# Attention outputs with queries as rows: P blocks stationary, V with a ones column moving, division per row, PE turns into the mix

## The chip, the cores and the metric

The kernel runs one decoder layer on one Trainium2 chip, on 8 cores; each core computes one of the eight sequences and the cores do not talk to each other. The metric is the device time of the slowest core, in microseconds (us). Some executions in this case were in a second, slower state: the cores of one die (cores 0 to 3 or 4 to 7) showed a lower granted clock and the time grew (one run of the kernel before took 3652.38 us with a clock of 0.81 on cores 4 to 7, beside 3125.60 us in the same job). Such runs are told as slow here and compared with nothing.

Names used below: PE is TensorE (matmuls), PEld its weight loads, DVE VectorE, ACT ScalarE, POOL GpSimd. "N" is the number of columns that a matmul streams. "FoX" is the forgetting attention, "SWA" the sliding-window attention. The "granted clock" is the share of its full speed at which PE was allowed to run, as the trace records it. A "bank" is a piece of PSUM, the memory that PE writes its sums to.

## The reference, cut to what matters

```python
D_MODEL = 2048; BATCH = 8; SEQ = 2048; HEAD_DIM = 128      # per core: one sequence of 2048
# 8 FoX heads (causal, all earlier keys), 8 SWA heads (window 128, 2 kv heads, a sink logit)

def forgetting_attention(q, k, v, log_f):
    cum = cumsum(log_f)
    for i in range(S // 128):                               # blocks of 128 queries
        s = q_i @ k[:end].T * d**-0.5 + cum_q - cum_k       # causal mask
        out_i = softmax(s) @ v[:end]

def sliding_window_sink_attention(q, k, v, sinks):
    # each 128-query block reads its own and the previous key block
    p = softmax(concat([s, sink]))[..., :-1]
    out = p @ v

def reference(x, c, ...):
    h = rmsnorm(x) * (1 + sc) + sh;  proj = h @ w_in         # q, k, v of both groups, forget gates
    mix = concat([fox, swa]) @ w_out
    x = x + gt_a * rmsnorm(mix)
    y = square(relu((rmsnorm(x) * ...) @ w_up)) @ w_down     # the MLP, d_ff = 8192
    return x + gt_m * rmsnorm(y)
```

## The kernel before: the parts that the change touches

Every operation is recorded by small helpers (`pe`, `act`, `tt`, `cp`), which put semaphores where one engine's operation depends on another's. Each engine gets its operations in the order in which they were recorded. `F.fill(n)` records about n matmuls of other work (the projections of later heads) in between, so that PE has something to do while DVE and ACT make probabilities.

Scores are made with keys as rows: `P[k, q]`. In the kernel before, V is stationary and P moves, so an output tile has the head dimension as rows, which is the form that `mix` and the output projection want. The denominators come from a second matmul, with a matrix of ones as the stationary operand.

```python
    def pv(st):                                      # FoX, one step: 128 keys x up to 512 queries
        ...
        pe([mm(ob(c0, TS), v, pp, kb == 0, kb == nkb - 1), mm(db(c0, TS), ones(), pp, kb == 0, kb == nkb - 1)],
           [v, pp, ones()], [ob(), db()])
        if kb == nkb - 1:                            # the tile is done: divide
            os = accs[1]
            act(rr(), db(), AF.Ln)
            cp(os(), ob())
            act(rr(), rr(), AF.Exp, scale=-1.0)
            tt(mix(h, slice(j * TS, j * TS + TS)), os(), rr(), ALU.mult)

        for kb in range(16):                         # SWA, one pass of 4 heads, 16 blocks of queries
            sexp(kb, 0)                              # ACT: P from the scores of two heads
            sexp(kb, 1)
            if late:
                late()                               # normalise the block before: ACT Ln, Exp; DVE product
            F.fill(tot / 32)
            if kb + 1 < 16:
                sqk(kb + 1, 0)                       # PE: the next block's scores
                sqk(kb + 1, 1)
            F.fill(tot / 32)
            late = spv(kb)                           # PE: P.V and denominators; DVE: + sink
        late()
```

The scores of FoX use three PSUM banks in rotation (`SF`) and run three steps ahead of P.V; the scores of SWA use two (`SB`).

The softmax here doesn't subtract the row's maximum and nothing guards it: scores larger than these inputs give would overflow.

## Time and profile before

| | before |
|---|---|
| median of the first 3 runs | 3128.81 us (3125.04 to 3580.78; the highest is a slow run) |
| profiled run | 3126.5 us; spans of the cores 3109.0 to 3124.7 us |
| PE busy | 93% of the span |
| MLP from its first matmul (mean of the cores) | 1822.7 us |

The first lines are from the page of the kernel before: the span, the busy time of the engines, and the chain of work that ended last (the operations that each had to wait for the one before, followed back from the end).

```profile
span 3124.7 us, 38905 instructions; the slowest of 8 cores (3109.0 to 3124.7 us)
PE 2913.8 (93%) x15016; PEld 1375.2 (44%) x15016; DVE 928.1 (30%) x1489; ACT 748.4 (24%) x1224; POOL 469.1 (15%) x614
PE 82%; DVE 5%; DMA 4%; ACT 4%; issue 3%; POOL 1%; SPq 0%; DVEq 0%; ACTq 0%; POOLq 0%
```

So PE bounds this kernel. The next lines are a table of stretches of the kernel before: each row is a stretch of time, its length, the busy time of each engine with the number of instructions, and then the granted clock of PE as a share of full speed, the share of DMA time, and GB/s. The rows are FoX heads 0 and 1, the two SWA passes, FoX heads 2 to 7, and the MLP.

```profile
core 3: us, PE busy (x) PEld busy (x) DVE busy (x) ACT busy (x) POOL busy (x), PEclk, DMA share, GB/s
269.90:596.10 326.20, 290.20 (x1656) 138.85 (x1653) 147.97 (x244) 112.07 (x200) 25.36 (x48) 0.91 0.49 86
596.10:715.60 119.50, 116.72 (x849) 76.39 (x848) 50.01 (x78) 72.61 (x131) 8.12 (x16) 0.99 0.39 66
715.60:1081.60 366.00, 334.68 (x2009) 168.31 (x2007) 196.15 (x343) 184.47 (x309) 29.37 (x49) 0.96 0.46 84
1301.60:3124.70 1823.10, 1774.81 (x8205) 803.76 (x8203) 323.41 (x476) 219.32 (x365) 255.78 (x350) 0.99 0.53 104
```

The SWA passes are the densest stretch of the attention: PE is busy for 116.7 of 119.5 us. The timeline of the kernel before shows why (start, duration, engine, operation with output and input tiles and shapes; a number in brackets is idle time before it, and what ended it). One block of SWA:

```profile
start us, us, engine line op out<-in xcount [idle before <-releaser]
605.93 1.03 PE L387 MATMUL bank<-hT,ring_70 128*128 128x512 bf16 x4
606.71 0.69 DVE L407 TENSOR_TENSOR mix<-bank,qrot 128x512 bf16<-128x512 f32 x1 [1.54 <-ACT qrot L404]
607.22 0.28 PE L387 MATMUL bank<-Pb_102,vts 128*128 128x256 bf16 x1
...
608.00 0.27 PE L387 MATMUL bank<-Pb_99,ones 128*128 128x256 bf16 x1
608.11 1.03 PE L387 MATMUL bank<-hT,ring_70 128*128 128x512 bf16 x4
608.38 0.69 DVE L407 TENSOR_TENSOR rr<-bank,esink 128x512 f32<-128x512 f32 x1 [0.97 <-PE bank L387]
```

P·V begins at 607.22, the last denominator matmul at 608.00, and at 608.11 PE is already on a projection (`hT`, `ring`). The division happens on DVE and ACT beside it, and nothing on PE waits for it. Matmuls overlap, so their durations do not add up; read their starts: N=256 matmuls start every 0.11 us, each shown as 0.27 us long.

### The profile page before, as it was taken

How to read it: one execution, taken by the hardware profiler on the slowest of the kernel's cores; microseconds unless marked ns; L12 is line 12 of the kernel's file. 1: busy time of each engine (PE TensorE's matmuls, PEld its weight loads, DVE VectorE, ACT ScalarE, POOL GpSimd, SP SyncE). 2: the span in 40 equal slices, each digit the busy share in tenths (PEclk: the TensorE clock that was granted, in tenths of full speed). 3: DMA queues.
4: the chain of work that ended last, by engine and by line, in shares of the span. 5: the costliest groups of instructions: out<-in, count | busy, mean ns of one | idle time of the engine just before them, and what ended most of it. 6: DMA issues, size and time to landing. Idle time of an engine off the chain costs nothing.

```text
span 3124.7 us, 38905 instructions; the slowest of 8 cores (3109.0 to 3124.7 us)
## 1 busy us (share of the span) xinstructions
PE 2913.8 (93%) x15016; PEld 1375.2 (44%) x15016; DVE 928.1 (30%) x1489; ACT 748.4 (24%) x1224; POOL 469.1 (15%) x614
## 2 busy tenths in 40 slices
PE   2799989999999899999999999999999999999993
PEld 1336533466444344444444444444444444444441
DVE  1323445345555456642111000000233211000005
ACT  1312333454555435532111000000111111000000
POOL 1010000000001155520000011111100000111114
PEclk9899989999999899999999999999999999999996
DMA  9855545433646324354444455555788544444455
GB/s 185 215 90 104 101 75 88 78 61 59 112 85 102 77 95 157 127 130 74 78 78 74 82 100 95 96 92 96 162 189 191 92 75 78 77 75 77 78 99 197
DMA packets 99782, 327.92 MB, mean 105 GB/s; under 512 B 12144, under 2 KB 12272, under 8 KB 93200
## 3 DMA queue, kind: packets, MB, share of 16 engines
q0 software_dynamic: 58896, 213.97, 41.6%
q1 hardware_dynamic: 40704, 111.46, 10.2%
q8 instruction: 122, 2.00, 0.3%
q14 instruction: 60, 0.49, 0.1%
HBM read 497.32 MB, written 42.01 MB: 173 GB/s over the span
## 4 chain that ended last, share of the span: by engine, by line
PE 82%; DVE 5%; DMA 4%; ACT 4%; issue 3%; POOL 1%; SPq 0%; DVEq 0%; ACTq 0%; POOLq 0%
PE bank L387 82%; DVE bank L407 1%; POOL acc_209 L407 1%; DMA xstA<-xP 1%; DMA xstB<-xP 1%; DMA rmod_87<-wMA 1%; ACT acc_208 L404 1%; DVE mixF L412 1%; ACT rr L404 1%; DMA cfb_82<-crow 1%; ACT qrot L404 1%; DMA rsh_90<-wMB 0%; DVE bank L412 0%; DVE sq_207 L412 0%; DVE acc_208 L412 0%
## 5 line engine op out<-in xcount | busy, mean ns | idle before, releaser
L418 DVE TENSOR_SCALAR bank<-bank 128x512 f32<-128x512 f32 x256 | 166.1, 695 | 638.4 <-PE bank L387 638.4
L421 DVE COPY mixF<-bank 128x512 f32<-128x512 f32 x64 | 41.3, 686 | 842.8 <-PE bank L387 842.8
L387 PE MATMUL bank<-mix,rung_130 128*128 128x512 bf16 x1024 | 226.2, 379 | 0.0
L387 PE MATMUL bank<-mix,rung_127 128*128 128x512 bf16 x1024 | 226.2, 379 | 0.0
L387 PE MATMUL bank<-mix,rung_128 128*128 128x512 bf16 x1024 | 226.2, 379 | 0.0
L387 PE MATMUL bank<-mix,rung_129 128*128 128x512 bf16 x1024 | 226.2, 379 | 0.0
L404 ACT ACTIVATE sq_206<-bank 128x512 f32<-128x512 f32 x30 | 17.9, 598 | 792.9 <-DVE mixF L421 792.9
L387 PEld LDWEIGHTS bank<-mix,rung_129 128*128 128x128 bf16 x1024 | 100.2, 98 | 121.5 <-issue 1.1
L387 PEld LDWEIGHTS bank<-mix,rung_127 128*128 128x128 bf16 x1024 | 100.3, 98 | 120.7
L387 PEld LDWEIGHTS bank<-mix,rung_128 128*128 128x128 bf16 x1024 | 100.4, 98 | 120.7
L387 PEld LDWEIGHTS bank<-mix,rung_130 128*128 128x128 bf16 x1024 | 99.9, 98 | 121.5 <-issue 0.6
L407 DVE TENSOR_TENSOR bank<-bank,cfb_82 128x512 f32<-128x512 f32 x192 | 117.3, 629 | 85.2 <-PE bank L387 80.6
L387 PE MATMUL bank<-hT,ring_69 128*128 128x512 bf16 x512 | 139.6, 404 | 3.2 <-DVE sq_207 L412 3.2
L387 PE MATMUL bank<-hT,ring_71 128*128 128x512 bf16 x384 | 101.7, 394 | 0.4 <-DVE kT_73 L421 0.4
L407 POOL TENSOR_TENSOR acc_208<-acc_208,sq_206 128x512 f32<-128x512 f32 x62 | 78.6, 1267 | 113.1 <-ACT sq_206 L404 113.0
L407 DVE TENSOR_TENSOR bank<-bank,cfb_80 128x512 f32<-128x512 f32 (+3 forms) x128 | 73.5, 594 | 39.2 <-PE bank L387 39.2
L407 POOL TENSOR_TENSOR acc_209<-acc_209,sq_207 128x512 f32<-128x512 f32 x62 | 78.3, 1262 | 45.0 <-ACT sq_207 L404 43.1
L387 PE MATMUL bank<-qT_93,kT_94 128*128 128x512 bf16 (+3 forms) x160 | 57.4, 359 | 24.3 <-DVE bs L421 14.2
L387 PEld LDWEIGHTS bank<-hT,ring_69 128*128 128x128 bf16 x512 | 51.0, 103 | 61.3 <-issue 16.9
L387 PE MATMUL bank<-qT_72,kT_73 128*128 128x512 bf16 (+3 forms) x160 | 57.1, 359 | 18.9 <-DVE bs L421 8.8
L387 PE MATMUL bank<-hT,ring_68 128*128 128x512 bf16 x256 | 67.1, 394 | 1.1 <-DVE kT_73 L421 1.1
L387 PE MATMUL bank<-hT,ring_67 128*128 128x512 bf16 x192 | 58.9, 393 | 0.0
(759 smaller groups left out, 4803.5 us busy)
## 6 DMA issues: line engine op xcount, KB each, us to landing
rung_127<-wU POOLq DMA_DIRECT2D x32, 512.0 KB, 5.3
rung_128<-wU POOLq DMA_DIRECT2D x32, 512.0 KB, 5.3
rung_129<-wU POOLq DMA_DIRECT2D x32, 512.0 KB, 5.2
rung_130<-wU POOLq DMA_DIRECT2D x32, 512.0 KB, 5.4
rung_127<-wD POOLq DMA_DIRECT2D x32, 512.0 KB, 5.2
rung_128<-wD POOLq DMA_DIRECT2D x32, 512.0 KB, 5.3
rung_129<-wD POOLq DMA_DIRECT2D x32, 512.0 KB, 5.3
rung_130<-wD POOLq DMA_DIRECT2D x32, 512.0 KB, 5.7
```

What stands on the lines that cost most here:

```text
L387: ins = e.matmul(o, lhsT=l, rhs=rh, start=st, stop=sp)
L404: return P.op("act", lambda e: e.activation(out=out.ap, in_=in_.ap, func=func, **kw), r, [out])
L407: return P.op(eng, lambda e: e.tensor_tensor(out=out.ap, in0=a.ap, in1=b.ap, op=op), [a, b], [out])
L412: return P.op(eng, lambda e: e.scalar_tensor_tensor(out=out.ap, in0=a.ap, scalar=sc, in1=b.ap, op0=op0, op1=op1), r, [out])
L418: return P.op(eng, lambda e: e.tensor_scalar(out=out.ap, in0=a.ap, scalar1=sc, scalar2=None, op0=op), r, [out])
L421: return P.op("dve", lambda e: e.tensor_copy(out=out.ap, in_=a.ap), [a], [out])
```

## The change

The intent is to make a stream of P·V serve for the denominators too. A block of P (128 keys by 128 queries) becomes the stationary operand, and V with an added column of ones moves (N=129). The output then has queries as rows, its column 128 is the denominator, and the division is by one number per row. That saves the whole denominator matmul. The price is that outputs lie with queries as rows, so a matmul with the identity must turn each 128x128 block before it goes to `mix`.

The core of the diff (cut: the V buffers get rows of 129, the ones columns are set, two small buffers move):

```diff
+    def outp(bk, o, add=None):
+        v = bk().re(bk.h[:, 0:258].rearrange("p (a d) -> p a d", a=2))
         ...
+        if add is not None:
+            tt(r, den, add, ALU.add)
+            den = r
+        P.op("dve", lambda e: e.reciprocal(out=r.ap, in_=den.ap), [den], [r])
+        tt(o, v.re(v.ap[:, :, 0:128]), r.re(r.ap.unsqueeze(2).broadcast_to([128, 2, 128])), ALU.mult)
+
+    def turn(on, bk):
+        pe([mm(bk(a * 128, a * 128 + 128), on(a), ident(), True, True) for a in range(4)], [on(), ident()], [bk()])

     def pv(st):                                   # FoX
-        pe([mm(ob(c0, TS), v, pp, ...), mm(db(c0, TS), ones(), pp, ...)], ...)
-        ... act Ln, cp, act Exp, tt mult
+        for x in range(2):
+            mms = [mm(bk(a * 129, a * 129 + 129), p(slice((2 * x + a) * 128, (2 * x + a) * 128 + 128)), v, ...) ...]
+            if d == 2 * x + 1:
+                outp(bk, on(slice(2 * x, 2 * x + 2)))
+        if d == 3:
+            def turned():                         # recorded one step later
+                bk = banks[SF[St.sb % 3]]         # takes a score bank
+                St.sb += 1
+                turn(on, bk)
+                cp(mix(h, slice(j * TS, j * TS + TS)), bk())
+            tail.append(turned)

         def spv(n):                               # SWA
-            ... V stationary and ones stationary, N=256; + sink
+            for pair in range(2):
+                ... mm(bk(a * 129, a * 129 + 129), p(slice(c, c + 128)), v, ...)
+                outp(bk, on(slice(2 * pair, 2 * pair + 2)), esink(...))
             def norm():                           # this is late()
-                act(rb(), rb(), AF.Ln)
-                act(rb(), rb(), AF.Exp, scale=-1.0)
-                tt(mix(...), ob(), rv, ALU.mult)
+                bk = banks[SB[St.sb % 2]]
+                St.sb += 1
+                turn(on, bk)
+                act(mix(...), bk(), AF.Copy)
```

The loop over SWA's blocks is the same as before. `late()` still stands where it stood.

More of the change, by code (lines that the diff above doesn't have):

```diff
@@ L373, in program @@
     accs = [B["acc0"], B["acc1"]]
+    onb = [B["on0"], B["on1"]]
+    rc = B["rc"]
     WO = [B[f"WO{i}"] for i in range(16)]
@@ L471, in program @@
         cf = 0
+        rc = 0
     PJ = [0, 1]
@@ L475, in program @@
     SF = [2, 3, 5]
-    OB = [4, 5]
-    DB = 6
+    OF = [4, 6]
+    OS = [4, 5, 6]
     MB = 7
@@ L558, in g_fm, with v_part, v_ones @@
             yield 4
+    def v_part(dst, b0):
+        d = dst(slice(b0, b0 + 2))
+        return d.re(dst.h[:, b0:b0 + 2, :, 0:128])
+    def v_ones(dst):
+        d = dst()
+        ap = dst.h[:, :, :, 128]
+        P.op("dve", lambda e: e.memset(ap, 1.0), [], [d])
     def g_v(slots, bp, dst, rel, add=None):
@@ L573, in g_v @@
                     src = bk()
-                    src = src.re(src.ap.rearrange("p (a d) -> p a d", a=2))
+                    src = src.re(src.ap.rearrange("p (a e d) -> p a e d", a=2, e=2))
+                    d = v_part(dst, 2 * bp)
                     if add is None:
-                        cp(dst(slice(2 * bp, 2 * bp + 2)), src)
+                        cp(d, src)
                     else:
-                        tt(dst(slice(2 * bp, 2 * bp + 2)), src, add().re(add.h[:].unsqueeze(1).broadcast_to([128, 2, 256])), ALU.add)
+                        av = add.h[:].rearrange("p (e d) -> p e d", e=2)
+                        for a in range(2):
+                            tt(d.re(d.ap[:, a]), src.re(src.ap[:, a]), add().re(av), ALU.add)
                 yield 4
@@ L646, in vpair @@
         s = [R1.acq(("A", i)), R1.acq(("A", i + 1))]
+        if dst is not vX:
+            v_ones(dst)
         if bias:
@@ L665, in svpair @@
         cp(bsv(), bk(0, 256))
+        v_ones(vts)
         for bp in range(8):
@@ L807, in wave_out @@
         b = bank_set(t)
+        if t == 0:
+            v_ones(vX)
         act(lf(slice(t * TS, t * TS + TS), p=(0, 8)), b[2](p=(0, 8)), AF.Copy)
@@ L810, in wave_out @@
             src = b[3 + i]()
-            src = src.re(src.ap.rearrange("p (a d) -> p a d", a=2))
-            d = vX(slice(4 * t + 2 * i, 4 * t + 2 * i + 2))
+            src = src.re(src.ap.rearrange("p (a e d) -> p a e d", a=2, e=2))
+            d = v_part(vX, 4 * t + 2 * i)
             if i:
@@ L968, in expo @@
         steps[st] = (p, c0)
+    def outp(bk, o, add=None):
+        v = bk().re(bk.h[:, 0:258].rearrange("p (a d) -> p a d", a=2))
+        i = (St.rc % 4) * 2
+        St.rc += 1
+        r = rc(slice(i, i + 2))
+        den = v.re(v.ap[:, :, 128])
+        if add is not None:
[5 more added lines that the diff above has]
+        pe([mm(bk(a * 128, a * 128 + 128), on(a), ident(), True, True) for a in range(4)], [on(), ident()], [bk()])
+    tail = []
     def pv(st):
@@ L972, in pv @@
         p, c0 = steps.pop(st)
-        nkb = 4 * j + 4
-        ob = banks[OB[0]]
-        db = banks[DB]
-        v = V_OF[h](kb, slice((h % 2) * 128, (h % 2) * 128 + 128))
-        pp = p(slice(c0, TS))
-        pe([mm(ob(c0, TS), v, pp, kb == 0, kb == nkb - 1), mm(db(c0, TS), ones(), pp, kb == 0, kb == nkb - 1)],
-           [v, pp, ones()], [ob(), db()])
-        if kb == nkb - 1:
-            os = accs[1]
-            act(rr(), db(), AF.Ln)
-            cp(os(), ob())
-            act(rr(), rr(), AF.Exp, scale=-1.0)
-            tt(mix(h, slice(j * TS, j * TS + TS)), os(), rr(), ALU.mult)
+        v = V_OF[h](kb, h % 2)
+        d = kb - 4 * j
+        for x in range(2):
+            bk = banks[OF[x]]
+            mms = [mm(bk(a * 129, a * 129 + 129), p(slice((2 * x + a) * 128, (2 * x + a) * 128 + 128)), v, kb == 0 and a == 0,
+                      a == 1 and d == 2 * x + 1) for a in range(2) if 2 * x + a >= d]
+            if mms:
+                pe(mms, [v, p(slice(c0, TS))], [bk()])
+            if d == 2 * x + 1:
+                on = onb[j % 2]
+                outp(bk, on(slice(2 * x, 2 * x + 2)))
[6 more added lines that the diff above has]
+            tail.append(turned)
     LA = 3
@@ L1015, in fox @@
             F.fill(w)
+            t = tail.pop(0) if tail else None
             pv(L[i])
+            if t:
+                t()
             if i + LA < n:
@@ L1019, in fox @@
             F.fill(w)
+        while tail:
+            tail.pop(0)()
     SPB = Pb
@@ L1048, in spv @@
         def spv(n):
-            St.ob += 1
-            ob = banks[OB[St.ob % 2]]
-            db = banks[DB]
-            mms = []
-            rd = [ones()]
-            for bk, is_den in ((ob, False), (db, True)):
-                for pair in range(2):
-                    o = bk(pair * 256, pair * 256 + 256)
-                    ov = o.re(o.ap.rearrange("p (a w) -> p a w", a=2))
-                    first = True
+            on = onb[n % 2]
+            for pair in range(2):
+                bk = banks[OS[St.ob % 3]]
+                St.ob += 1
+                mms = []
+                rd = []
+                for a in range(2):
                     for kb, lo in ((n - 1, 128), (n, 0)):
@@ L1062, in spv @@
                         p, W = info[(kb, pair)]
-                        pa = p(slice(0, 2 * W))
-                        rh = pa.re(pa.ap.rearrange("p (a w) -> p a w", a=2)[:, :, lo:lo + 128])
-                        v = ones() if is_den else vts(kb, slice(g * 128, g * 128 + 128))
-                        mms.append(mm(ov, v, rh, first, kb == n))
-                        rd += [pa, v]
-                        first = False
-            pe(mms, rd, [ob(), db()])
-            es = esink(slice(4 * g, 4 * g + 4))
-            rb = (rr, qrot)[n % 2]
-            rv = rb().re(rb.h[:].rearrange("p (a w) -> p a w", a=4))
-            tt(rv, db().re(db.h[:, :].rearrange("p (a w) -> p a w", a=4)),
-               es.re(es.ap.unsqueeze(2).broadcast_to([128, 4, 128])), ALU.add)
-            def norm():
-                act(rb(), rb(), AF.Ln)
-                act(rb(), rb(), AF.Exp, scale=-1.0)
-                tt(mix(slice(8 + 4 * g, 12 + 4 * g), slice(n * 128, n * 128 + 128)),
-                   ob().re(ob.h[:, :].rearrange("p (a w) -> p a w", a=4)), rv, ALU.mult)
+                        v = vts(kb, g)
+                        c = a * W + lo
+                        mms.append(mm(bk(a * 129, a * 129 + 129), p(slice(c, c + 128)), v, a == 0 and lo == (128 if n else 0),
+                                      a == 1 and kb == n))
+                        rd += [p(slice(0, 2 * W)), v]
+                pe(mms, rd, [bk()])
+                outp(bk, on(slice(2 * pair, 2 * pair + 2)), esink(slice(4 * g + 2 * pair, 4 * g + 2 * pair + 2)))
+            def norm():
+                bk = banks[SB[St.sb % 2]]
+                St.sb += 1
+                turn(on, bk)
+                act(mix(slice(8 + 4 * g, 12 + 4 * g), slice(n * 128, n * 128 + 128)),
+                    bk().re(bk.h[:, :].rearrange("p (a w) -> p a w", a=4)), AF.Copy)
             return norm
@@ L1410, in build @@
     buf("xstA", MIX, [16, TS], F32)
-    buf("cosT", MIX + 2 * 4096, [S], F32)
-    buf("sinT", MIX + 4 * 4096, [S], F32)
-    buf("vY", MIX + 6 * 4096, [16, 256], BF16)
+    buf("cosT", MIX + 2 * 4096 - 128, [S], F32)
+    buf("sinT", MIX + 4 * 4096 - 128, [S], F32)
+    buf("vY", MIX + 6 * 4096 - 128, [16, 2, 129], BF16)
     buf("hT", H, [NT, KC, TS], BF16)
@@ L1423, in build @@
     buf("Cf", o, [S], F32)
-    o = buf("vts", o, [16, 256], BF16)
+    buf("vts", o, [16, 2, 129], BF16)
+    o += 8192 + 128
     buf("lf", o, [S], F32)
-    buf("vZ", o, [16, 256], BF16)
-    o = buf("skT", o, [2, S], BF16)
+    buf("vZ", o, [16, 2, 129], BF16)
+    buf("skT", o, [2, S], BF16)
+    o += 8192 + 128
     for i in range(2):
@@ L1436, in build @@
         o = buf(nm, o, [S], BF16)
-    o = buf("vX", o, [16, 256], BF16)
-    assert o == RS + 65536
+    buf("vX", o, [16, 2, 129], BF16)
+    o += 8192 + 128
     for i in range(2):
@@ L1443, in build @@
     o = buf("stage", o, [TS], F32)
-    o = buf("rr", o, [TS], F32)
+    buf("rr", o, [TS], F32)
     o = buf("qrot", o, [TS], F32)
@@ L1452, in build @@
     for nm, n, dt in (("identF", 8, F32), ("sel4", 4, F32), ("sinks", 8, F32), ("esink", 8, F32), ("bfg", 2, F32), ("cc", 16, F32),
-                      ("shb", 16, BF16), ("bq", 8, F32), ("bqb", 2, BF16), ("bs", 10, F32), ("bsw", 10, F32)):
+                      ("shb", 16, BF16), ("bq", 8, F32), ("bqb", 2, BF16), ("bs", 10, F32), ("bsw", 10, F32), ("rc", 16, F32)):
         buf(nm, o, [n], dt)
@@ L1483, in build @@
         o = buf(f"acc{i}", o, [TS], F32)
+    for i in range(2):
+        buf(f"on{i}", o - 2048 + 1024 * i, [4, 128], BF16)
     assert BASE + o <= nc.sbuf_usable_end, (BASE + o, nc.sbuf_usable_end)
```

## The prediction

> **What bounds it now.** The page gives PE 93% busy of 3125 us and the chain of waits 82% on PE. By windows, the MLP (after about 1300 us) runs PE at 100% and is not touched. The change acts between 270 and 1082 us: eight forgetting-attention (FoX) heads, with two sliding-window (SWA) passes at about 585-715 us. Heads 3 to 6 take 55-60 us each, about 52 us of it matmul streaming; heads 0, 1 and 7 have more beyond streaming (about 30, 41 and 21 us). The SWA passes stream almost without a gap: one block takes 3.46 us on the timeline.
>
> **Removed (PE).** Start-to-start intervals in the trace: N=512 216 ns, N=256 109 ns, N=128 56 ns, also where every matmul loads new weights; N=1 matmuls with new weights come every 25 ns. So weight loads hide, and N=129 should cost about 56 ns (estimate). [...]
> - FoX, per head: P·V and denominators stream 34,816 columns, 14.7 us. New: 136 matmuls of N=129, 7.7 us, and 16 turns of N=128, 0.9 us. Saved 6.1 us a head, 49 us in all.
> - SWA, per block: eight N=256 (0.87 us) become eight N=129 and four turns (0.67 us): 6 us in all.
> ACT loses two activations of 0.63 us per output tile; DVE work is about equal.
>
> **Added: waits.** [...]a turn at the head of PE's order stops everything behind it.
> - SWA: the turn is issued directly after the block's own P·V matmuls, with no fill between. It needs, for two pairs serially on DVE: add sink, reciprocal, product. In the trace, two dependent tiny DVE operations start 0.26 us apart; DVE starts 0.11 us after a matmul's end; a 256-column product is about 0.42 us (estimate from 0.69 for 512, 0.16 for 1). That makes about 2.4 us from the first P·V matmul, where PE is done after 0.45: idle about 2 us a block, 32 blocks, +64 us. The old normalisation ran beside the fill.
> - FoX: the turn is put off by one step, so its input is mostly ready. But it takes one of three score banks in rotation. The score step two later must wait for an exponential queued behind the turn's copy: about 2.5 us (copy 0.69, subtraction 0.63, exponential 0.65, hand-overs), where PE has about 1.5 us of work. About 1 us idle per tile in heads 2 to 7, some 20 us; heads 0 and 1 have enough fill.
>
> **Sum.** FoX -49 +20, and some unrealised: about -26. SWA -6 +64: +58. Net about +32 us: 3160 us, range 3115 to 3198. Chances: faster 0.03, same 0.82, slower 0.15.
>
> **What would show it.** Timeline of SWA: P·V, then about 2 us without PE, then the turns; block period 5.3 us instead of 3.46; both passes 185-195 us instead of 131. PE waits name DVE products. N=129 start to start 56 ns. FoX heads 3 to 6 shorter by 1-5 us, with a short PE wait a few steps after each tile's end. MLP unchanged, its granted clock 1.00.
>
> **What would make it wrong.** N=129 slower than 56 ns (+15 ns would cost about 20 us); granted clock falling in SWA because of the idle time (slower); short DVE forms faster, or FoX bank waits absent (towards 3120); FoX latency-bound, so nothing of its 49 us arrives (towards 3190).

## The result, and the profile after

The changed kernel takes 3207.45 us (median of 4 runs, 3205.23 to 3209.59). The ratio to the kernel before is 1.0255, with a 95% interval of 1.0235 to 1.0276: slower by more than 2%. Ratios in this document are the mean time of one kernel's fast runs over the mean of the other's fast runs of the same rounds, so they are not quite the ratio of the medians quoted beside them.

From the page of the kernel after: the same lines as before, and from its groups of instructions (count, then busy time and mean ns of one, then idle time of the engine just before them and what ended it) the group of the turns.

```profile
span 3203.5 us, 40593 instructions; the slowest of 8 cores (3181.8 to 3203.5 us)
PE 2902.5 (91%) x15720; PEld 1399.3 (44%) x15720; DVE 943.2 (29%) x1725; ACT 694.5 (22%) x1128; POOL 469.1 (15%) x614
PE 80%; DVE 8%; DMA 4%; issue 4%; ACT 3%; POOL 1%; DVEq 0%; SPq 0%; POOLq 0%; ACTq 0%
L389 PE MATMUL bank<-ident,on 128*128 128x128 bf16 x256 | 27.1, 234 | 75.3 <-DVE on L409 73.4
```

PE idles for 75.3 us just before turns, 73.4 us of it until DVE has made `on`, the divided outputs. Which stretch that is, the windows of the kernel after show (the same four stretches):

```profile
core 3: us, PE busy (x) PEld busy (x) DVE busy (x) ACT busy (x) POOL busy (x), PEclk, DMA share, GB/s
271.00:593.50 322.50, 277.12 (x1798) 141.84 (x1796) 152.78 (x279) 102.50 (x184) 25.92 (x50) 0.91 0.58 88
593.50:823.50 230.00, 156.31 (x977) 88.26 (x976) 55.97 (x207) 57.01 (x100) 7.88 (x15) 0.81 0.23 37
823.50:1160.90 337.40, 299.49 (x2434) 177.75 (x2434) 199.94 (x409) 156.58 (x261) 29.05 (x48) 0.96 0.48 90
1379.90:3203.50 1823.60, 1775.49 (x8205) 804.11 (x8203) 323.28 (x476) 219.25 (x365) 255.83 (x350) 0.99 0.54 104
```

FoX heads 2 to 7 became shorter (366.0 to 337.4 us), the MLP did not move, and the SWA passes went from 119.5 to 230.0 us. Two things changed there: PE is idle for 74 us, and its granted clock is 0.81 instead of 0.99. Averaged over the eight cores of each profiled run, by the starts of the first matmuls of each stage:

| stretch | before, us | after, us | difference |
|---|---|---|---|
| up to FoX head 0 | 268.5 | 270.7 | +2.2 |
| FoX heads 0 and 1 | 323.8 | 322.5 | -1.3 |
| the two SWA passes | 118.9 | 224.4 | +105.5 |
| FoX heads 2 to 6 | 293.5 | 267.5 | -26.0 |
| FoX head 7 | 70.0 | 66.4 | -3.6 |
| the rest | 2042.0 | 2042.4 | +0.4 |

The timeline of one SWA block after the change:

```profile
start us, us, engine line op out<-in xcount [idle before <-releaser]
655.47 0.63 PE L389 MATMUL bank<-vts,Pb 128*128 128x129 bf16 x8
655.98 0.16 DVE L409 TENSOR_TENSOR rc<-bank,esink 128x2 f32<-128x2 f32 x1 [6.89 <-PE bank L389]
656.24 0.17 DVE L1001 RECIPROCAL rc<-rc 128x2 f32<-128x2 f32 x1
656.51 0.42 DVE L409 TENSOR_TENSOR on<-bank,rc 128x256 bf16<-128x256 f32 x1
657.04 0.16 DVE L409 TENSOR_TENSOR rc<-bank,esink 128x2 f32<-128x2 f32 x1
657.30 0.17 DVE L1001 RECIPROCAL rc<-rc 128x2 f32<-128x2 f32 x1
657.57 0.42 DVE L409 TENSOR_TENSOR on<-bank,rc 128x256 bf16<-128x256 f32 x1
658.25 0.38 PE L389 MATMUL bank<-ident,on 128*128 128x128 bf16 x4 [2.16 <-DVE on L409]
658.47 1.63 PE L389 MATMUL bank<-hT,ring 128*128 128x512 bf16 x4
```

P·V is done 0.6 us after it begins. Then PE waits 2.16 us for six short DVE operations, three for each pair of heads, one after the other. The projection that could fill the gap is recorded behind the turn, so it starts at 658.47. That much was predicted. What was not in the predicted time is in the last line: those four N=512 matmuls take 1.63 us on the timeline, where the same line before took 1.03. The clock was low (0.50 from 658.75 us on).

The granted clock in slices of 3.41 us, as the trace records it, for a stretch of the kernel after:

```profile
core 3: us, PE busy (x) PEld busy (x) DVE busy (x) ACT busy (x) POOL busy (x), PEclk, DMA share, GB/s
634.86:638.27 3.41, 2.51 (x15) 1.33 (x16) 0.54 (x2) 1.33 (x3) 0.00 (x0) 1.00 0.95 140
638.27:641.69 3.41, 1.26 (x16) 0.89 (x14) 1.50 (x6) 0.35 (x1) 0.00 (x0) 1.00 0.06 11
641.69:645.10 3.41, 3.41 (x10) 1.18 (x8) 0.00 (x0) 1.19 (x2) 0.00 (x0) 0.50 0.00 0
645.10:648.51 3.41, 1.36 (x12) 0.73 (x10) 1.63 (x6) 0.60 (x1) 0.00 (x0) 1.00 0.00 0
648.51:651.93 3.41, 2.58 (x10) 1.22 (x11) 0.47 (x2) 0.60 (x1) 0.00 (x0) 0.50 0.01 2
651.93:655.34 3.41, 3.41 (x12) 0.92 (x10) 0.00 (x0) 1.19 (x2) 0.00 (x0) 0.50 0.00 0
```

In this trace the record of PE's clock has only two values, 1.00 and 0.50, in 318 pieces each over the eight cores; the shortest piece is 3.41 us long, and in the SWA passes every piece is a whole number of such slices long. (The 0.81 above is their mean over the passes on core 3; the mean of the cores is 0.83.) A slice at full clock in which PE was busy for 1.26 us (or 1.36) is followed by a slice at half clock; the one with 2.51 us is not. At half clock a slice with 2.58 us busy was still followed by another at half clock. At half clock the N=512 matmuls of the fill and of the scores start every 0.43 us instead of 0.216.

### The profile page after: what moved, and what is told of

Same layout as the page of the kernel before. It is cut to its first block, busy times and chain, and to the rows that moved or that the text cites. A ratio compares the mean times of both kernels' runs of the same rounds, so it can differ in the third digit from the quotient of the medians.

```text
span 3203.5 us, 40593 instructions; the slowest of 8 cores (3181.8 to 3203.5 us)
## 1 busy us (share of the span) xinstructions
PE 2902.5 (91%) x15720; PEld 1399.3 (44%) x15720; DVE 943.2 (29%) x1725; ACT 694.5 (22%) x1128; POOL 469.1 (15%) x614
## 4 chain that ended last, share of the span: by engine, by line
PE 80%; DVE 8%; DMA 4%; issue 4%; ACT 3%; POOL 1%; DVEq 0%; SPq 0%; POOLq 0%; ACTq 0%
PE bank L389 80%; DVE bank L409 1%; POOL acc L409 1%; DVE on L409 1%; DMA xstA<-xP 1%; DMA xstB<-xP 1%; ACT Pb L406 1%; DMA rmod<-wMA 1%; DVE sq L414 1%; ACT acc L406 1%; DVE mixF L414 1%; DVE bank L414 1%; ACT sq L406 0%; DVE rc L1001 0%; DMA rsh<-wMB 0%
## 5 line engine op out<-in xcount | busy, mean ns | idle before, releaser
L389 PE MATMUL bank<-mix,rung 128*128 128x512 bf16 x4096 | 884.9, 379 | 0.0
L389 PE MATMUL bank<-a,rung 128*128 128x512 bf16 x4096 | 884.4, 379 | 0.0
L389 PEld LDWEIGHTS bank<-mix,rung 128*128 128x128 bf16 x4096 | 400.8, 98 | 484.3 <-issue 1.7
L389 PEld LDWEIGHTS bank<-a,rung 128*128 128x128 bf16 x4096 | 400.8, 98 | 483.3
L389 PE MATMUL bank<-hT,ring 128*128 128x512 bf16 x1536 | 423.5, 403 | 4.2 <-DVE sq L414 4.1
L406 ACT ACTIVATE Pb<-bank,Ctok 128x512 bf16<-128x512 f32 (+1 forms) x320 | 193.2, 623 | 359.9 <-DVE bank L409 341.1
L409 POOL TENSOR_TENSOR acc<-acc,sq 128x512 f32<-128x512 f32 x180 | 225.1, 1266 | 216.4 <-ACT sq L406 212.3
L389 PE MATMUL bank<-mix,WO 128*128 128x512 bf16 x1024 | 232.7, 380 | 15.6 <-ACT sq L406 14.7
L409 DVE TENSOR_TENSOR bank<-bank,cfb 128x512 f32<-128x512 f32 (+1 forms) x320 | 190.3, 614 | 78.5 <-PE bank L389 75.2
L389 PE MATMUL bank<-ring,hT 128*128 128x256 bf16 x1280 | 186.3, 294 | 7.1 <-DVE sq L414 3.2
L389 PE MATMUL bank<-ident,on 128*128 128x128 bf16 x256 | 27.1, 234 | 75.3 <-DVE on L409 73.4
```

The lines of the kernel that those rows point to most:

```text
L389: ins = e.matmul(o, lhsT=l, rhs=rh, start=st, stop=sp)
L406: return P.op("act", lambda e: e.activation(out=out.ap, in_=in_.ap, func=func, **kw), r, [out])
L409: return P.op(eng, lambda e: e.tensor_tensor(out=out.ap, in0=a.ap, in1=b.ap, op=op), [a, b], [out])
```

## The experiments

Theory A: the turn at the head of PE's order leaves PE idle some 2.3 us a block, and the lower clock is a consequence of that idle time. Rival B: the new kind of work (narrow matmuls, P as stationary operand, short DVE operations) costs the time and the clock, wherever it stands. The two differ on what happens when the same work is done without the wait, and when the wait is kept but PE is busy. The second question is what FoX gave, and why.

A table of the fast runs first. "Before" is the mean of that kernel's fast runs of the same job; the passes and the clock are means over the eight cores of the profiled run.

| kernel | fast runs, us (number) | before, us | ratio | SWA passes, us | clock there |
|---|---|---|---|---|---|
| changed | 3207.4 (4) | | 1.0255 | 224.4 | 0.83 |
| e1_swa_before | 3105.8 (3 of 4) | 3128.4 | 0.9928 | 119.7 | 0.99 |
| e2_turn_late | 3105.9 (4) | 3128.4 | 0.9928 | 125.1 | 0.97 |
| e3_turn_half | 3147.3 (2 of 4) | 3128.4 | none | 164.4 | 0.98 |
| e4_dummy8 | 3171.7 (3 of 4) | 3128.4 | 1.0139 | 188.7 | 1.00 |
| e5_split_turn | 3192.6 (1 of 4) | 3128.3 | none | 210.8 | 0.85 |
| e6_late_foxact | 3093.5 (4) | 3128.3 | 0.9889 | 124.4 | 0.98 |
| e7_late_order | 3086.7 (4) | 3128.3 | 0.9867 | 118.3 | 0.97 |
| e8_dummy2 | 3177.1 (1 of 2) | 3129.8 | none | 196.4 | 0.96 |
| e9_dummy4 | 3172.7 (1 of 2) | 3129.8 | none | 193.5 | 0.97 |
| e10_work01 | 3099.3 (2 of 4) | 3129.8 | 0.9902 | 118.6 | 0.97 |
| e11_bs_act | 3085.4 (4) | 3129.8 | 0.9857 | 117.8 | 0.98 |

All outputs are right. Where no ratio stands, too few fast runs were left for an interval. The runs come from three jobs on different chips (e1 to e4; e5 to e7; e8 to e11), where the kernel before took 3128.4, 3128.3 and 3129.8 us; in the last, one of its six fast runs, 3149.5 us, has a lower clock on cores 0 to 3 and lifts the mean by 4 us.

### e1_swa_before: FoX changed, SWA as before

```diff
         def spv(n):
-            for pair in range(2): ... P stationary, outp, turn
+            ... V stationary, ones stationary, N=256 (the kernel before's spv)
```

> The change's FoX part alone; the sliding-window (SWA) part as before (V stationary, a ones matmul for the denominators, Ln and Exp). Both theories put the loss into the SWA passes (traces: 120 us before, 230 us after, from the first SWA block to head 2), so both expect about 110 us less than the changed kernel: 3097 us, which would be 32 us faster than before, what the traces show FoX to have gained. If FoX carried a part of the loss, the time would lie above 3110 us.

Measured: 3105.8 us, ratio 0.9928 (0.9908 to 0.9947). The loss is gone with the SWA part, so all of it sat there, and the FoX part alone is a gain of 23 us (3128.4 minus 3105.8). It is less than the 32 us that one core's trace of the changed kernel had suggested. In e1's own profile, as a mean over the cores and against the kernel before, heads 0 and 1 gave 1.0 us, heads 2 to 6 21.6 us and head 7 3.4 us, and the stretch before the first head took 3.2 us more.

### e2_turn_late: the SWA turn moved behind the fill

```diff
             sexp(kb, 0); sexp(kb, 1)
-            if late:
-                late()
             F.fill(tot / 32)
             if kb + 1 < 16: sqk(kb + 1, 0); sqk(kb + 1, 1)
             F.fill(tot / 32)
+            if late:
+                late()
             late = spv(kb)
         # in norm(): the turn goes to the third output bank, not to a score bank
-                bk = banks[SB[St.sb % 2]]
+                bk = banks[OS[St.ob % 3]]
```

> The changed kernel with one thing moved: in SWA the turn of a block is issued after the next block's scores and both fills, just before the next P.V, into the third output bank. Theory A (the turn at the head of PE's order leaves PE idle some 2.3 us a block, and the granted clock falls because of that idle time): idle gone, granted clock in the SWA stretch 0.97 or more, the two passes about 115 us, in all about 3095 us. Theory B (the narrow matmuls with P stationary, or the kind of work, cost the time and the clock): the passes stay near 230 us, in all about 3205 us.

Measured: 3105.9 us, 0.9928 (0.9911 to 0.9946). Every matmul, DVE operation and copy of the changed kernel is still done; only their order and one bank differ. The passes fall from 224.4 to 125.1 us and the clock comes back to 0.97. This decides between A and B: the kind of work does not cost the time. PE's waits in the SWA passes, longest first, in the kernel after

```profile
PE bank L389 <- DVE on L409: 72.4, 32, 2.9
```

and in e2 (us in total, times, longest):

```profile
PE bank L389 <- DVE on L409: 5.1, 4, 2.2
PE bank L389 <- ACT Pb L406: 1.1, 3, 0.4
```

The window of e2 over its two passes, on its slowest core (columns as in the tables of stretches above):

```profile
596.60:721.60 125.00, 117.99 (x968) 70.30 (x975) 56.16 (x207) 51.87 (x99) 7.88 (x15) 0.97 0.38 65
```

It is 11 us slower than the 3095 us expected; the passes take 125 us where the streaming at full clock would be some 113 (the 118.9 us before, less 6). Experiment e7 takes that up.

### e3_turn_half, e8_dummy2, e9_dummy4, e4_dummy8: how much idle time the clock bears

e3 has the turn after the first fill; the others leave the turn where the change put it and add 2, 4 or 8 useless N=512 matmuls before it, into the output bank that is free, which are overwritten by the next block:

```diff
             # e4; range(4) in e9, range(2) in e8
+            db = banks[OS[St.ob % 3]]
+            p, W = info[(n, 0)]
+            v = vts(n, g, slice(0, 128))
+            pe([mm(db(0, 2 * W), v, p(slice(0, 2 * W)), True, True) for _ in range(8)], [v, p(slice(0, 2 * W))], [db()])
             def norm(): ...
```

> As e2, but the turn comes after the first fill only (four N=512 matmuls, 0.86 us of cover). Theory A: about 1.4 us of idle time is left a block, 45 us in all; 3140 us if the clock recovers with it, 3165 to 3175 us if the clock stays near 0.8. Theory B: 3205 us. Tells how much idle time a block can have before the clock falls.

> The changed kernel with eight useless N=512 matmuls (1.73 us at full clock) between a block's P.V and its turn, into the free output bank; the turn waits as long as before, but PE is busy while it does. Theory A: the granted clock in the SWA stretch comes back to 0.95 or more, the block period to about 5.4 us, in all about 3158 us, though PE does more work. Rival (the clock falls because of the kind of work, or because the load is high): it stays near 0.8, in all 3207 us or more.

> As e4 with two useless matmuls instead of eight (0.43 us of the wait covered): some 1.9 us of idle time is left a block. In the changed kernel 2.3 us left a granted clock of 0.81 over the two passes, in e3 1.46 us left 0.98. If the idle share decides gradually, the clock lies between, about 0.85 to 0.92; if there is a sharp edge below 1.9 us, it stays at 0.81. Looked at in the profile only.

> As e8 with four useless matmuls (0.87 us covered): some 1.45 us of idle time is left a block, as much as in e3, but with the turn in its old place and bank. If the idle time is what counts and not the place of the turn, the clock is 0.97 or more, as in e3, and the total about 3160 us. If the turn's place or bank counts, it stays near 0.81.

e3 came out at a clock of 0.98, as theory A has it when the clock recovers, with 3147.3 us for the 3140 us expected: some 52 us of idle time were left and not 45.

e4 measures the clock by itself: the turn waits as before, PE does 256 matmuls more than in the changed kernel, and the program is 36 us faster (3171.7 against 3207.4 us; the passes 188.7 against 224.4). Extra work made it faster because it held the clock (1.00 in the passes, 0.83 in the changed kernel). The windows of e4 over its two passes:

```profile
597.10:785.20 188.10, 166.84 (x1212) 95.54 (x1230) 55.98 (x207) 54.79 (x99) 7.86 (x15) 1.00 0.26 44
```

Its total is 14 us above the 3158 us expected, because a block took 5.9 us (188.7 us over 32 blocks) and not 5.4; the clock, which the experiment was for, came as theory A has it. The windows of e9 and e8 over their passes, in this order:

```profile
595.20:788.70 193.50, 146.02 (x1104) 84.56 (x1103) 55.98 (x207) 55.64 (x100) 7.83 (x15) 0.97 0.26 43
596.80:791.90 195.10, 134.23 (x1041) 78.94 (x1040) 55.98 (x207) 55.74 (x100) 7.85 (x15) 0.96 0.25 43
```

e9 was expected at 0.97 or more and about 3160 us; the clock is 0.97, the one fast run 3172.7 us (the useless matmuls themselves are 128 times 0.216 us, 28 us of PE time that e3 does not have). So the amount of idle time counts, and not the turn's place or bank: e3 and e9 have nearly the same idle time (52.1 and 51.5 us before turns) and nearly the same clock (0.98 and 0.97) in spite of different places. e8 came out at 0.96, a little above the expected 0.85 to 0.92. So most of the clock is regained, 0.96 after 0.83, by filling as little as 0.43 us of each wait.

### e5_split_turn: the same wait in two pieces

```diff
-                turn(on, bk)
+                for u in range(2):
+                    pe([mm(bk(a * 128, a * 128 + 128), on(a), ident(), True, True) for a in (2 * u, 2 * u + 1)],
+                       [on(slice(2 * u, 2 * u + 2)), ident()], [bk()])
```

> The changed kernel with the SWA turn in two parts that wait apart: two matmuls when the first pair is divided, two when the second is. PE does the same work and waits for the same last input, so its idle time per block stays (some 2.2 us), but it comes in two pieces of about 1.2 and 1.0 us. If the length of a single gap decides the granted clock, it comes back to 0.95 or more in the SWA stretch and the total to about 3160 us. If the idle share decides, it stays near 0.8 and the total near 3205 us.

Measured: 3192.6 us (one fast run), clock 0.85 in the passes. This is nearer to the second outcome than to the first, but neither number was hit.

```profile
595.00:807.50 212.50, 150.87 (x976) 84.49 (x974) 55.95 (x207) 56.91 (x100) 7.82 (x15) 0.85 0.24 40
```

With gaps of 1.2 us (median), shorter than e8's 1.9, the clock is lower than e8's. The following table puts these runs in the order of the idle time before turns, worked out from the starts of the matmuls (the start of the first turning matmul minus the start of the matmul before it and that one's streaming time at full clock), summed over the two passes, mean of the cores:

| kernel | idle before turns, us | median gap, us (gaps) | clock |
|---|---|---|---|
| changed | 77.7 | 2.32 (32) | 0.83 |
| e5_split_turn | 71.3 | 1.2 (64) | 0.85 |
| e8_dummy2 | 64.9 | 1.89 (32) | 0.96 |
| e3_turn_half | 52.1 | 1.46 (32) | 0.98 |
| e9_dummy4 | 51.5 | 1.46 (32) | 0.97 |
| e4_dummy8 | 24.9 | 0.60 (32) | 1.00 |

In these six runs the clock follows the sum, not the length of a single gap. That it is the busy share of one 3.41 us slice that decides is what the slices above suggest, and the kept traces show where the edge lies. Take every slice from the first FoX head to the last, on all cores of the twelve profiled runs without e10 (which had a disturbed clock), and count in it the streaming time of the matmuls: N times 216/512 ns at full clock, twice that at half clock, overlaps once. Of 20158 slices at full clock, all 1251 with less than 1.0 us of streaming were followed by a slice at half clock, and all 18256 with 1.4 us or more by one at full clock; in between, both happened. At half clock, 748 of the 749 slices with less than 2.2 us were followed by another at half clock, and all 1665 with 2.7 us or more by one at full clock. In the SWA passes the clock fell after 22 slices per core in the changed kernel, after 18 in e5, 5.6 in e8, 4.0 in e9, 3.1 in e3 and 1.0 in e4. So what counts is how often so little work falls into one slice.

### e6_late_foxact and e7_late_order: the rest of the waits

e6 is e2 with FoX's copy of the turned tile on ACT; e7 also moves SWA's copy on ACT behind the next block's exponentials.

```diff
         # e6, FoX
-                cp(mix(h, slice(j * TS, j * TS + TS)), bk())
+                act(mix(h, slice(j * TS, j * TS + TS)), bk(), AF.Copy)
         # e7, SWA: norm() only turns, and returns the copy, which the loop records after the two sexp
             sexp(kb, 0); sexp(kb, 1)
+            if copy:
+                copy()
             ...
             if late:
-                late()
+                copy = late()
```

> As e2 (late SWA turn), and in FoX the copy of the turned tile is taken from DVE to ACT, so that the next score's subtraction no longer stands behind it. If the FoX part's small waits come from the score bank that the turn takes and from the copy in DVE's order (as the prediction said), PE's waits for exponentials in heads 2 to 6 fall from 15 us to some 5 us and the total by about 10 us, to 3095 us. If not, it stays at 3106 us.

> As e6, and in SWA the ACT copy of the turned block is issued after the next block's two exponentials instead of before them. In e2 PE still waited 8 us for exponentials and 5 us for DVE in the two passes (125 us where streaming alone gives about 113). If the order on ACT is the cause, the passes take about 115 us and the total is about 10 us below e6, some 3085 us, the fastest of all. If not, it equals e6.

e6: 3093.5 us, 12.4 us below e2, about the size expected, but not for the reason alone that was given. PE's waits for exponentials in heads 2 to 6 were to fall from 15 to some 5 us; by the view of waits, each run read over its own heads 2 to 6, they fell from 15.3 us (e2) to 11.1 us (core 3; cores 1 and 5 agree within 0.5 us). By starts of matmuls, the idle time before the first two score matmuls after each turn fell in these heads from 17.8 us (e2) to 12.7 us (mean of the cores), nearly all of it at the second one, from 10.1 to 5.6 us. The time of the stages fell by 5.6 us in heads 0 and 1, 4.2 us in heads 2 to 6 and 1.3 us in head 7. So taking the copy off DVE helps in all of FoX; that the score bank is the main reason is not shown.

e7: 3086.7 us, 6.8 us below e6; the passes take 118.3 instead of 124.4 us, so the order on ACT was the cause of e2's missing microseconds. The view of waits hardly shows them: the 8 us for exponentials in the expectation come from a window that reached into FoX heads 2 and 3, and in the passes alone e2 has 1.1 us. By starts of matmuls (mean of the cores), PE was idle for 7.4 us before the score matmuls of the passes in e2 and for 0.6 us in e7, which is about the whole gain. In the first pass, P·V of one block starts 3.4 us after that of the block before, on average (before: 3.5; changed: 6.8). e7 beats both kernels: 0.9867 (0.9851 to 0.9882) of the kernel before.

### e10_work01 and e11_bs_act: why FoX heads 0 and 1 gave almost nothing

```diff
         # e10, in FoX's P.V: useless matmuls into unused columns of the output bank, heads 0 and 1
+                if h < 2 and c0 == 0:
+                    mms.append(mm(bk(258, 512), ones(), p(slice(0, 254)), False, False))
         # e11, the bias column of the rotary stripes
-        cp(bs(slice(i, i + 1)), bk(0, 1))
+        act(bs(slice(i, i + 1)), bk(0, 1), AF.Copy)
```

> As e7, with useless matmuls added to P.V in FoX heads 0 and 1 alone (two of N=254 in every full step, 56 steps, about 12 us of PE time; as much as the change took away there). If these two heads are bound by waits and not by PE's work, as the missing gain there suggests, the time of the two heads grows by less than 5 us (total under 3092 us). If PE bounds them, by about 12 us, to 3099 us. The extra sums go to unused columns of the output banks; the result stays right.

> As e7, with the copy of the rotary bias column (the wait that costs PE 22 us in heads 0 and 1) moved from DVE to ACT. If it waits there for DVE's queue, PE's waits on it fall and the two heads gain 5 to 15 us (3075 to 3082 us in all). If ACT's queue is as late, or other waits take over, it stays at 3087 us.

In e10 two of four runs were slow, and the two fast ones (3092.5 and 3106.0 us) differ; in the profiled one, the slower, the clock over the whole span was 0.967 and 0.965 on cores 6 and 7, beside 0.973 to 0.976 on the others. So the total is not used; in the two heads the disturbance does not show: the clock of core 7 there was 0.93, beside 0.92 in e7 (its core 6). They take 319.5 us against 315.9 in e7: 3.6 us longer for about 12 us more PE work. These heads are bound mostly by waits, and PE work taken from them is mostly not gained.

e11 was to show which wait. PE's wait for the bias column was about 21 us in these heads and stayed at 21.1 us on ACT; the two heads came down from 315.9 to 311.1 us, but the whole program is at 3085.4 us against 3086.7, with intervals that overlap widely. So moving it out of DVE's order did not help; ACT's order may be as late. Why the column is late stays open. The trace of e11 gives a lead that was not tested: before six of the ten copies ACT sat idle for 0.95 us until a DVE product (`sq`) that reads the same buffer `bs` was done.

## Why the prediction was wrong, point by point

It predicted 3160 us (3115 to 3198) and the kernel takes 3207; it gave "slower by over 2%" a chance of 0.15, and that is what came.

- **PE bounds the kernel; the MLP does not change.** Right: 1822.7 and 1823.4 us.
- **N=129 with new weights costs about 56 ns.** Right: 57 to 58 ns is the median interval from start to start in the kernel after, at full clock; for N=128 (the turns) it is 55 ns. The odd width and offset cost next to nothing, so the narrow matmuls did save the PE time they were to save: removed work was not the failed step.
- **SWA: the turn waits, about 2 us a block, +64 us.** The mechanism was right: what is recorded behind the turn waits with it (2.16 us in the block above), and e2 moves the turn and the loss is gone. The size was somewhat off: 2.32 us in the median, 77.7 us in all. The projected DVE chain was sound (tiny operations 0.26 us apart, the 256-column product 0.42 us), but in some blocks a projection's copy of 0.69 us stands ahead of it on DVE, as at 646.1 us of the trace, where the wait is 2.9 us. With the clock on top, the block period was 6.8 us and not 5.3.
- **The failed step: "SWA -6 +64: +58" with the clock left at 1.00.** The two passes were to grow by 58 us and grew by 105.5 us. The sum charged the wait at its own length. With the wait, PE's clock also fell to 0.50 for whole 3.41 us slices (22 times per core in the passes), so that PE's remaining work took longer as well. e4 removes that part alone: 36 us. Then 118.9 (before) - 6 + 77.7 + 36 makes 227 us, an estimate from these numbers, where 224.4 was measured. The prediction had the falling clock among the things that could make it wrong, but put no number on it, and its upper limit of 3198 us left no room for it.
- **FoX: -49 +20, about -26.** The total came close, 23 us by e1, but by luck: the terms were not right, and their errors cancelled. The bank wait was to cost 1 us a tile at the second score step after each turn. By starts of matmuls on core 3, PE was idle for 0.56 us there (10.7 us over 19 tiles of heads 2 to 6), while the first score step waited too (7.4 us), which was not foreseen. Not all of this is new: the idle time before all score matmuls of these heads was 16.2 us in the kernel before and 22.4 us in the one after (mean of the cores), so the change added only about 6 us there, where the prediction's share for five of six heads was some 17. This fits the 26.0 us that these heads gave of the 30.5 us taken from PE (five times 6.1). On the other side, heads 0 and 1, which were to give their full 12 us ("have enough fill"), gave 1.3 us: e10 shows that they are bound mostly by waits.
- **"PE waits name DVE products."** Right: 72.4 us on `on` in the view of waits.

## What to carry to other kernels

When a step that used to end on DVE and ACT now needs PE again, ask what stands behind that new PE operation in PE's order: record it after enough independent work to cover the whole chain that feeds it. Here moving one call and one bank (e2) turned a loss of 2.5% into a gain of 0.7%, and removing the copies from the way made it 1.3% (e7). And charge a repeated PE wait at more than its length (here by 36 us for 77.7 us of waits, as e4 shows): look at how much PE would still stream in each 3.41 us, because below 1.0 us the clock fell every time in these runs (1251 slices of 1251), for all the work in the slice that followed.
